# Three of four gate projections by seven products, norm's weights spread by TensorE, and three token blocks side by side

## The chip, the cores and the metric

The kernel runs on one core of one Trainium2 chip. The metric is the time of one execution on the device in microseconds, as the median of several. A core has the engines TensorE (matmuls, with the weight load as a step of its own), VectorE, ScalarE, GpSimd and SyncE, which here issues all DMAs. TensorE writes to PSUM, eight banks of 128 x 512 fp32 in this kernel; everything else lies in SBUF or in DRAM.

## The reference, cut to what matters

One decoder layer on 1024 tokens of width 1024. A norm, one wide input projection, two token mixers (attention, and a chunked state space scan, here SSD), a gated merge:

```
h = x * rsqrt(mean(x*x) + EPS) * norm_w                      # 1024 x 1024
q, k, v, z_a, xBC, z_s, dt, gates = split(h @ w_in)          # z_s: 2048 columns, four groups of 512
y_a = diff_attention(q, k, v) * silu(z_a)
y_s = group_rms_norm(ssd(silu(conv(xBC)), softplus(dt)) * silu(z_s))
merged = sigmoid(g_a) * (y_a @ w_proj_attn) + sigmoid(g_s) * (y_s @ w_proj_ssd)
out = x + merged @ w_out
```

The change concerns z_s, the 1024 x 2048 projection whose silu gates the scan's output, and norm_w.

## The kernel before

**Number format.** Every fp32 operand of a large matmul is split into a high and a low part, and a product is three matmuls, high-high, high-low and low-high (`steps3`, L557). For a weight block this means a ScalarE copy to the high part and a subtraction for the low part on VectorE or GpSimd, called a split below (`w_splits`, L424).

**Order.** No engine's order is left to a scheduler. A planner in the kernel's own Python (`Plan`, L79) holds an estimated time for each engine, runs generators as tasks, and so writes the instructions of all engines in one fixed order; each engine then works off its own list and waits where its data are not there. `bulk` (L1757) gives the order of TensorE's large pieces, `ORDER1` (L351): z0, dt, z1, then pairs of conv blocks (c), pairs of gate blocks (g), z2 and z3 between them, then eight attention heads (h), the remaining gates, the three merge products and the last projection. The SSD scan runs beside it as 32 chunks (four groups of eight), one every SLOW = 40 planned us in the front part and every PACE = 20 later.

**A plain z.** `ssd_proj_z(g)` (L1200) holds the eight weight blocks of 128 rows x 512 columns in eight of nine weight slots, and takes the eight token blocks one after the other: 8 row blocks x 3 matmuls into one PSUM bank, then silu on ScalarE and a store (`z_evac`, L1210). A weight slot is given back only after its use by the last token block.

**Seven products.** The pairs c and g already use Strassen-Winograd's form with seven half-size products instead of eight (`front_pair`, L1069; `ORDER`, L1456): the token halves of h are combined into four summed forms once (`form_evac`, L586), the weight quarters into sums on GpSimd (`pair_splits`, L452), and the products are added up in SBUF and PSUM. A pair's matmul has weights as the stationary and 512 tokens as the moving operand.

**Buffers.** Four raw buffers for loaded weights, nine weight slots, 17 big and 16 middle ones in SBUF, eight PSUM banks. SSD may hold up to ten of the middle ones. The loader (`w_loads`, L380) takes buffers and issues loads in the list's order, so that a load that can't get its buffer holds up all later ones; ScalarE and VectorE work off the splits in the same order.

**The start.** `start` (L1778) loads the first x block in two halves, norm_w as two broadcasts of 512 columns to 128 partitions (`nwb`), and four weight blocks. `prep_h` (L632) takes each x block through the norm (VectorE multiplies by the row's scale and nwb, L659), eight transposes on TensorE, and `h_evac` writes the high and the low part.

Of the kernel before, what the change touches and what calls it, by code (L numbers as in the profile page):

```python
# [27 lines left out]
C_B = C_XBC + 2048  # L28
C_C = C_B + 512
C_ZS = 7168  # L30
# [109 lines left out]
def tile_hybrid_layer(ctx: ExitStack, tc: tile.TileContext, x, norm_w, w_in, q_norm_w, k_norm_w,  # L140
# [22 lines left out]
    cv_d = dram.tile([3072, S], F32, name="cv_d")  # L163
    z_d = dram.tile([GROUPS, S, 512], F32, name="z_d")
    t_d = dram.tile([12, 2, P, S], F32, name="t_d")

# [182 lines left out]

    CONV = (16, 20, 0, 2, 4, 6, 18, 22, 8, 10, 12, 14)  # L350
    ORDER1 = [("z", 0), ("dt", 0), ("z", 1)]  # L351
    for i in range(12):
        ORDER1 += [("c", CONV[i])] + ([("g", i - 1)] if i % 2 else [])
        if i in ZF:
            ORDER1.append(("z", ZF[i]))
    FPAIRS = [i for i in ORDER1 if i[0] in "cg"]
    ORDER1.append(("setup", 0))
    for h in range(HEADS):
        ORDER1.append(("h", h))
        if h in ZH:  # L360
            ORDER1.append(("z", ZH[h]))

    wlist = []
    for kind, i in ORDER1:
        if kind in "cg":
            wlist.append(pair_w(w_in, 0, (C_XBC if kind == "c" else C_GATE) + i * P))
        elif kind != "setup":
            wlist += att_w(i) if kind == "h" else wide_w(w_in, C_ZS + i * 512) if kind == "z" else block_w(w_in, KB, C_DT, SH)
# [11 lines left out]
    def w_loads(lo, hi):  # L380
        for i in range(lo, hi):
            if isinstance(wlist[i], list) and isinstance(wlist[i][0], list):
                ks, raw, at = [], [], []
                for u in range(2):
                    for q in range(4):
                        ks.append((yield from pl.get(mids if u else raws)))
                    raw += [midt([P, 4, P], name=f"rawp{i}{q}") if u else
                            rpool.tile([P, 4, P], F32, tag="raw", name=f"rawp{i}{q}") for q in range(4)]
                    at += [load(raw[u * 4 + q], wlist[i][u][q // 2][:, :, q % 2 * P:(q % 2 + 1) * P]) for q in range(4)]
                raw_of[i] = (raw, ks, at)  # L390
                continue
            if isinstance(wlist[i], list):
                ks = yield from pl.get(raws, 4)
                raw = [rpool.tile([P, 4, P], F32, tag="raw", name=f"rawf{i}{q}") for q in range(4)]
                raw_of[i] = (raw, ks, [load(raw[q], wlist[i][q // 2][:, :, q % 2 * P:(q % 2 + 1) * P]) for q in (0, 1, 2, 3)])
                continue
# [27 lines left out]
    def w_splits():  # L424
        for i in range(len(wlist)):
# [5 lines left out]
            if isinstance(wlist[i], list):  # L431
                yield from pair_splits(*raw_of.pop(i), "G" if i < NFRONT else "V")
                continue
            k = yield from pl.get(ws)
# [17 lines left out]
    def pair_splits(raw, ks, at, eng):  # L452
# [33 lines left out]
        raws.give(ks[2], t)  # L486
        raws.give(ks[3], max(t, t22))

    def pairs_splits(raw, ks, at):
# [142 lines left out]
    def prep_h(t):  # L632
# [22 lines left out]
        pts = []  # L655
        nt = []
        for i in range(2):
# [400 lines left out]

    cv_at, z_at, ssd_n = {}, {}, {}

    def front_form(f, i):
# [5 lines left out]
    def front_pair(kind, b, last):  # L1067
# [6 lines left out]
        cell = {"kc": (yield from pl.get(mids)), "x": x, "ks": ks}  # L1074
        step = conv_step if kind == "c" else gate_step
        for n, (f, p) in enumerate(ORDER):
# [17 lines left out]
            w_done(ids[n])  # L1094
            pl.spawn(step(b, p, into[p], cell), pe_done())

# [10 lines left out]

    def gate_out(row, h, src, o, k, at):
        yield at
        at = act(o, src, AF.Tanh, at, scale=0.5)  # L1110
        t = at
        yield at
        at = load(gt_d[row * P:(row + 1) * P, h * 512:h * 512 + 512], o, at)
        mids.give(k, at)
        return t

    def gate_step(b, p, ps, cell):
        at = pe_done()
# [3 lines left out]
        elif p == 2:  # L1122
            k = yield from pl.get(mids)
            t = yield from gate_out(b, 0, ps, midt(name="go"), k, at)
            trs.give(kx, t)
        elif p == 4:
            c = cell["c"]
            at = tt(c, c, ps, ALU.add, max(at, cell["u", 7][2]))
            trs.give(ky, at)
            yield from gate_out(b + 1, 0, c, c, cell["kc"], at)  # L1130
        else:
# [5 lines left out]
            if p == 3:  # L1137
                trs.give(kz, at)
            yield from gate_out(b + (p == 5), 1, u, u, k, at)

# [59 lines left out]
    def ssd_proj_z(g):  # L1200
        ids = w_next(KB)
        for t in range(NT):
            k = yield from pl.get(trs, first=True)
            pm = mmt(f"pmz{g}{t}")
            yield from proj_tok(pm, t, ids, t == NT - 1)
            pl.spawn(z_evac(g, t, pm, k), pe_done())
            if g == 0 and t == 0:
                pl.spawn(consts())
# [15 lines left out]
    def ssd_core(g):  # L1224
# [532 lines left out]
    def bulk():  # L1757
        pl.spawn(ssd_all())
        pl.spawn(prepare())
        step = {"z": ssd_proj_z, "h": att_proj}  # L1760
        for kind, i in ORDER1:
            if kind in "cg":
                yield from front_pair(kind, i, (kind, i) == FPAIRS[-1])
            elif kind in step:
                yield from step[kind](i)
            else:
                yield from dt_proj() if kind == "dt" else att_setup()
        pl.spawn(fill())
        yield from gates()
        lag[:] = [0.0135, 2.5]  # L1770
        for c in range(3):
            yield from products(c)
        yield from final()

    kn = [mids.take() for _ in range(2)]
    nwb = [midt(name=f"nwb{i}") for i in range(2)]

    def start():  # L1778
        load_x(0)
# [11 lines left out]
        while len(h_at) < 2 * NT:  # L1791
            yield pl.t + 1.0
        for k in kn:
            mids.give(k, pl.t)

    def rest():
# [35 lines left out]
```

## Time and profile before

| | |
|---|---|
| median of 3 runs (lowest, highest) | 1624.73 us (1622.62, 1625.15) |
| the profiled execution's own time | 1625.04 us |
| its span in the trace | 1623.3 us |
| TensorE busy | 1589.2 us, 98% of the span |
| weight loads busy | 1330.2 us, 82% |
| VectorE, ScalarE, GpSimd busy | 1088.5, 915.1, 706.9 us |

The span runs from the first to the last instruction of one profiled execution; the own time holds 1.7 us around it. Busy time of TensorE is that of overlapping matmuls, so the pace of a stream is read from the starts of its matmuls and not from their durations. PE is TensorE, PEld its weight load, DVE VectorE, ACT ScalarE, POOL GpSimd, SP SyncE; a releaser is what an instruction waited for.

### The profile page before, as it was taken

The page shows a single profiled execution, that of the slowest core. Times are in us where ns is not written, and L with a number is a line of the kernel's source. Part 1 is how long each engine was busy: PE and PEld are TensorE (multiplying, and loading weights), DVE is VectorE, ACT ScalarE, POOL GpSimd, SP SyncE. Part 2 cuts the span into 40 slices and gives each one's busy share as a digit, 9 for nine tenths or more (in the row PEclk, how much of TensorE's full clock was granted, in tenths as well). Part 3 has the DMA queues.
Part 4 walks back from the last instruction along what each step waited for, and adds up shares of the span by engine and source line. Part 5 has one row for each costly group of instructions (what it writes and reads, how often), then busy time and mean ns, then how long its engine had stood idle before and what let it go on. Part 6 is the DMA issues. An engine that isn't in the chain of part 4 may idle for free.

```text
span 1623.3 us, 24344 instructions
## 1 busy us (share of the span) xinstructions
PE 1589.2 (98%) x8010; PEld 1330.2 (82%) x8010; DVE 1088.5 (67%) x2011; ACT 915.1 (56%) x2215; POOL 706.9 (44%) x847
## 2 busy tenths in 40 slices
PE   7999999999999999999989999999999999999999
PEld 5788888888788888887878888887887888888887
DVE  7836567537782576876767777876556577798831
ACT  7534447445563475786766777776666565352220
POOL 4315445334542543546475746464756433323000
PEclk9999999999999999999999999999999999999999
DMA  6213343533453461425163432433426397698941
GB/s 210 92 55 105 112 145 111 168 101 114 125 168 107 121 183 61 131 79 182 40 207 128 145 90 85 120 101 103 155 80 206 99 310 253 207 340 254 317 153 65
DMA packets 223804, 236.47 MB, mean 146 GB/s; under 512 B 15285, under 2 KB 155326, under 8 KB 223678
## 3 DMA queue, kind: packets, MB, share of 16 engines
q1 hardware_dynamic: 223678, 234.93, 45.6%
q8 instruction: 63, 1.03, 0.3%
q14 instruction: 63, 0.52, 0.1%
HBM read 164.48 MB, written 70.39 MB: 145 GB/s over the span
## 4 chain that ended last, share of the span: by engine, by line
PE 73%; DVE 3%; ACT 2%; POOL 2%; DMA 2%; issue 1%; SPq 0%; POOLq 0%; DVEq 0%; ACTq 0%
PE pma L199 18%; PE py L199 6%; PE pmz L199 5%; PE po L199 5%; PE pO L199 4%; PE pz L199 4%; PE px L199 4%; PE sc L199 4%; PE av L199 4%; PE fYc L199 3%; PE fXc L199 2%; PE pg L199 2%; PE pa L208 2%; PE fZc L199 2%; PE fYg L199 1%; PE pS L199 1%
## 5 line engine op out<-in xcount | busy, mean ns | idle before, releaser
L199 PE MATMUL pma<-w,hH 128*128 128x512 f32 x1024 | 345.2, 405 | 6.0 <-POOL w L233 5.4
L199 PEld LDWEIGHTS pma<-w,hH 128*128 128x128 f32 x1024 | 188.6, 189 | 40.9 <-POOL w L233 6.6
L199 PE MATMUL pma<-w,hL 128*128 128x512 f32 x512 | 206.8, 404 | 0.0
L199 PE MATMUL pmz<-w,hH 128*128 128x512 f32 x512 | 164.1, 398 | 0.7 <-ACT hH L225 0.7
L233 POOL TENSOR_TENSOR rawf<-rawf,rawf 128x512 f32<-128x512 f32 x54 | 71.6, 1326 | 166.4 <-DVE wp L233 87.8
L225 ACT ACTIVATE p<-p,nm 128x256 f32<-128x256 f32 (+7 forms) x128 | 98.6, 773 | 33.6 <-DVE nm L831 32.9
L225 ACT ACTIVATE w<-raw 128x512 fp32r<-128x512 f32 (+1 forms) x122 | 75.1, 626 | 75.0 <-DMA raw<-in_w_in_dram 28.7
L199 PEld LDWEIGHTS pmz<-w,hH 128*128 128x128 f32 x512 | 96.5, 190 | 20.6 <-ACT hH L225 1.1
L199 PEld LDWEIGHTS pma<-w,hL 128*128 128x128 f32 x512 | 96.8, 189 | 16.4
L233 POOL TENSOR_TENSOR w<-raw,w 128x512 fp32r<-128x512 f32 (+1 forms) x38 | 51.3, 1351 | 134.5 <-ACT w L225 120.7
L199 PE MATMUL fYc<-ft,wp 128*128 128x512 f32 x432 | 106.5, 392 | 0.7 <-DVE fu L233 0.7
L199 PE MATMUL pmz<-w,hL 128*128 128x512 f32 x256 | 101.4, 396 | 0.0
L199 PEld LDWEIGHTS fYc<-ft,wp 128*128 128x128 f32 x432 | 81.1, 189 | 17.9 <-DVE fu L233 1.1
L225 ACT ACTIVATE wp<-rawp 128x512 fp32r<-128x512 f32 x72 | 44.2, 626 | 84.1 <-POOL rawp L233 23.9
L233 DVE TENSOR_TENSOR wp<-rawf,wp 128x512 fp32r<-128x512 f32 x72 | 59.1, 837 | 34.7 <-ACT wp L225 34.7
L233 DVE TENSOR_TENSOR w<-raw,w 128x512 fp32r<-128x512 f32 (+1 forms) x84 | 65.1, 782 | 23.5 <-ACT w L225 23.3
L225 ACT ACTIVATE ab<-ab,nac 128x128 f32<-128x128 f32 x256 | 78.4, 392 | 1.7 <-POOL ab L1234 1.5
L199 PEld LDWEIGHTS av<-v,at 128*128 128x128 f32 x576 | 72.8, 191 | 6.5 <-ACT at L225 2.6
L265 POOL TENSOR_TENSOR rs<-rs,mhalf 128x4 f32<-128x4 f32 (+1 forms) x71 | 75.4, 1062 | 5.9
L225 ACT ACTIVATE wp<-rawf 128x512 fp32r<-128x512 f32 x108 | 65.9, 626 | 20.0 <-POOL rawf L233 16.4
L199 PE MATMUL av<-v,at 128*128 128x128 f32 x576 | 75.1, 275 | 1.7 <-ACT at L225 1.7
L831 DVE CUSTOM_DVE_ANT_0 p<-sc,maskb 128x512 f32<-128x512 f32 (+3 forms) x128 | 72.1, 584 | 6.2 <-PE sc L199 3.9
(299 smaller groups left out, 4217.8 us busy)
## 6 DMA issues: line engine op xcount, KB each, us to landing
raw<-in_w_in_dram SPq DMA_DIRECT2D x104, 256.0 KB, 3.6
rawf<-in_w_in_dram SPq DMA_DIRECT2D x72, 256.0 KB, 3.7
ab<-act_d SPq DMA_DIRECT2D x32, 512.0 KB, 4.9
cv_d<-cv SPq DMA_DIRECT2D x48, 256.0 KB, 2.1
t_d<-ts SPq DMA_DIRECT2D x24, 512.0 KB, 3.1
z_d<-zs SPq DMA_DIRECT2D x32, 256.0 KB, 2.0
xr<-cv_d SPq DMA_DIRECT2D x32, 256.0 KB, 3.0
zc<-z_d SPq DMA_DIRECT2D x32, 256.0 KB, 3.0
```

What stands on the lines that cost most here:

```text
L199: nc.tensor.matmul(o, lhsT=lhsT, rhs=rhs, start=start, stop=stop, **kw)
L208: nc.tensor.transpose(out=o, in_=i, identity=ident if idn is None else idn)
L225: nc.scalar.activation(o, i, f, **kw)
L233: (nc.vector if eng == "V" else nc.gpsimd).tensor_tensor(out=o, in0=a, in1=b, op=op)
L265: nc.gpsimd.tensor_tensor(out=dst, in0=dst, in1=mhalf[:, 0:cols], op=ALU.pow)
L831: nc.vector.tensor_tensor_reduce(out=p[:, j:e], in0=sc[i][:, 0:e - j], in1=maskb[:, S - n + j:S - n + e], scale=-1.0, scalar=nms[i - 1] if ...
```

## The change

z1, z2 and z3 are computed with seven products of 512 tokens x 512 rows x 256 columns each; z0 stays plain (`PLAIN`). Here the tokens are the stationary operand and 256 columns of the weights the moving one, since the result is wanted with tokens on partitions. A product's weight block comes as two halves of 256 rows (`tok_w`, `tok_splits`), 14 in all, from eight loads of which four go to raw and four to middle buffers. `tok_unit` runs the products, `tok_step` adds them up and stores. z2 and z3 come earlier in the order by two c pairs and one g pair each (`FRONT_ORDER`). PACE becomes 21. SSD starts a group when its z has been stored by the plan's time instead of when its stores are planned.

norm_w comes as two rows of 512 in one partition, and TensorE spreads them over the partitions by a matmul of full fp32 with a column of ones into two PSUM banks, which are held until all of h is made.

In z0 the last three token blocks run side by side: for each weight block three token blocks, in three banks.

Some parts that the diff also names are not used here (`za_d`, `v_d`, the kinds a and v).

```diff
-PACE = 20
+PACE = 21
-ZF, ZH = {5: 2, 9: 3}, {}
+FRONT_ORDER = "z0 d0 z1 c16 c20 g0 c0 c2 g2 z2 c4 c6 g4 c18 c22 g6 z3 c8 c10 g8 c12 c14 g10"
+PLAIN = (("z", 0),)
...
+    def tok_w(c0):
+        return tuple(w_in[kh * 512 + kp * 256:kh * 512 + kp * 256 + 256, c0 + r * 256:c0 + r * 256 + 256]
+                     .rearrange("(k p) c -> p k c", p=P) for kp in range(2) for kh in range(2) for r in range(2))
...
+            if isinstance(wlist[i], tuple) and len(wlist[i]) == 8:
+                ks = yield from pl.get(raws, 4)
+                raw = [rpool.tile([P, 2, 256], F32, tag="raw", name=f"rawt{i}{q}") for q in range(4)]
+                at = [load(raw[q], wlist[i][q]) for q in range(4)]
+                km = yield from pl.get(mids, 4)
+                raw += [midt([P, 2, 256], name=f"rawt{i}{q}") for q in range(4, 8)]
+                at += [load(raw[q], wlist[i][q]) for q in range(4, 8)]
...
+    def tok_splits(raw, ks, km, at):
+        a11, a21, a12, a22 = [[raw[q], raw[4 + q]] for q in range(4)]
+        kt = yield from pl.get(mids, 2)
...
+        for kp in range(2):
+            yield t0[kp]
+            t3.append(tt(s3[kp], a11[kp], a21[kp], ALU.subtract, t0[kp], "G"))
+            t1.append(tt(a21[kp], a21[kp], a22[kp], ALU.add, t0[kp], "G"))
+        u11 = yield from split(a11, t0, "V")
+        for kp in range(2):
+            t2.append(tt(a11[kp], a21[kp], a11[kp], ALU.subtract, max(t1[kp], u11[kp]), "G"))
+        yield from split(a11, t2, "V")
+        u12 = yield from split(a12, t0, "V")
+        for kp in range(2):
+            t4.append(tt(a12[kp], a12[kp], a11[kp], ALU.subtract, max(t2[kp], u12[kp]), "G"))
...
+        t = yield from split(s3, t3, "G")
...
+        t = yield from split(a21, t1, "V")
...
+        t = yield from split(a22, t0, "G")
...
+        t = yield from split(a12, t4, "G")
...
+        while "nwb" not in ready:
+            yield pl.t + 0.1
...
+    def tok_unit(kind, g, last):
+        ids = w_next(14)
...
+        for n, (f, p) in enumerate(ORDER):
+            for b in range(2 * ((into[p], 0) not in ps)):
+                k = yield from pl.get(trs, first=True)
+                ps[into[p], b] = (trt(f"t{into[p]}{kind}{g}{b}"), k)
+            for kp in range(2):
+                yield from w_need(ids[2 * n + kp])
+                if f[0] == "t":
+                    while any(("formed", t) not in ready for t in range(4, NT)):
+                        yield pl.t + 0.2
...
+                for j in range(4):
+                    b = j // 2
+                    while kp == 0 and p in BEFORE and (("c22", b) if p == 3 else (BEFORE[p], b)) not in cell:
+                        yield pl.t + 0.1
+                    o = ps[into[p], b][0][:, j % 2 * 256:j % 2 * 256 + 256]
+                    for kk in range(2):
+                        hf = front_form(f, 2 * kp + kk)
+                        yield from steps3(o, [a[:, j * P:(j + 1) * P] for a in hf], (wt[:, 0, kk], wt[:, 1, kk]),
+                                          kp + kk == 0 and p in (1, 6, 5) and j % 2 == 0, kp + kk == 2, skip_group_check=True)
+                    if kp and j % 2:
+                        pl.spawn(tok_step(kind, g, p, b, ps[into[p], b], cell), pe_done())
+                w_done(ids[2 * n + kp])
...
+    def tok_step(kind, g, p, b, bank, cell):
...
+        if p == 1:
+            k = yield from pl.get(mids)
+            c = midt(name=f"tc{b}")
+            cell["ct", b] = (c, k, act(c, ps, AF.Copy, at))
+        elif p in (6, 7):
...
+            cell[("u", p), b] = (u, k, tt(u, cell["ct", b][0], ps, ALU.add, at))
+        elif p == 2:
+            k = yield from pl.get(mids)
+            yield from out(ps, midt(name="to"), k, at, True)
+        elif p == 4:
+            c, k, t = cell["ct", b]
+            at = tt(c, c, ps, ALU.add, max(at, t, cell[("u", 7), b][2]))
+            trs.give(kb, at)
+            yield from out(c, c, k, at, False)
...
     def ssd_proj_z(g):
         ids = w_next(KB)
-        for t in range(NT):
+        for ts in ((0,), (1,), (2,), (3,), (4,), (5, 6, 7)):
...
-        while any(cv_at.get(i, INF) > pl.t for i in need) or any((g, t) not in z_at for t in range(NT)):
+        while any(cv_at.get(i, INF) > pl.t for i in need) or any(z_at.get((g, t), INF) > pl.t for t in range(NT)):
...
-    kn = [mids.take() for _ in range(2)]
-    nwb = [midt(name=f"nwb{i}") for i in range(2)]
+    kn, kb_ = [mids.take() for _ in range(2)], [trs.take() for _ in range(2)]
+    nwr = [midt([1, 512], name=f"nwr{i}") for i in range(2)]
+    nwb = [trt(f"nwb{i}") for i in range(2)]
+    one = const.tile([1, P], F32, name="one")
+    nc.gpsimd.memset(one, 1.0)
+
+    def norm_rows(t):
+        yield t
+        for i in range(2):
+            mm(nwb[i], one, nwr[i], True, True)
+        ready["nwb"] = pe_done()
...
-            load(nwb[i], norm_w[:, i * 512:i * 512 + 512].partition_broadcast(P).rearrange("p a d -> p (a d)"))
+            t = load(nwr[i], norm_w[:, i * 512:i * 512 + 512])
+        pl.spawn(norm_rows(t), t)
```

## Rows read from the trace of the kernel before

**Rows 1.** The page: each engine's busy us, share of the span, instructions.

```profile
PE 1589.2 (98%) x8010; PEld 1330.2 (82%) x8010; DVE 1088.5 (67%) x2011; ACT 915.1 (56%) x2215; POOL 706.9 (44%) x847
```

**Rows 2.** Waits of TensorE: total us, times, longest us.

```profile
PE pma L199 <- POOL w L233: 5.4, 3, 2.3
PE pO L199 <- DVE cv L241: 2.5, 1, 2.5
```

**Rows 3.** Timeline of z0 (start us, us): 28 rounds of three lie between.

```profile
40.38 0.61 PE L199 MATMUL pmz<-w,hH 128*128 128x512 f32 x2
...
59.42 0.61 PE L199 MATMUL pmz<-w,hH 128*128 128x512 f32 x2
```

**Rows 4.** Timeline of 256-column matmuls; tile view of their loads (ns min/median/max).

```profile
1615.39 0.88 PE L199 MATMUL po<-w,hH 128*128 128x256 f32 x6
...
1616.11 0.88 PE L199 MATMUL po<-w,hL 128*128 128x256 f32 x6
...
L199 PEld LDWEIGHTS po<-w,hH x204: 187/188/192, 1532.5 to 1619.8; 128*128 128x128 f32 x102
```

**Rows 5.** Groups of the pairs' weights; DMA issues with us to landing.

```profile
L225 ACT ACTIVATE wp<-rawf 128x512 fp32r<-128x512 f32 x108 | 65.9, 626 | 20.0 <-POOL rawf L233 16.4 <-PE pmz L199 2.6 <-DMA rawf<-in_w_in_dram 0.2
L233 DVE TENSOR_TENSOR wp<-rawf,wp 128x512 fp32r<-128x512 f32 x72 | 59.1, 837 | 34.7 <-ACT wp L225 34.7
L233 POOL TENSOR_TENSOR rawf<-rawf,rawf 128x512 f32<-128x512 f32 x54 | 71.6, 1326 | 166.4 <-DVE wp L233 87.8 <-issue 43.9 <-PE fYc L199 13.1
...
rawf<-in_w_in_dram SPq DMA_DIRECT2D x72, 256.0 KB, 3.7
```

**Rows 6.** Busy us in z2: PE, PEld, DVE, ACT, POOL; clock, DMA, GB/s.

```profile
301.50:350.20 48.70, 48.70 (x231) 40.66 (x230) 13.95 (x23) 24.07 (x47) 12.41 (x13) 1.00 0.38 121
```

**Rows 7.** Timeline of the start; busy us there (columns as in rows 6).

```profile
2.63 2.01 SPq L254 DMA_DIRECT2D raw<-in_w_in_dram  x4
3.56 0.63 ACT L225 ACTIVATE hL<-x 128x512 fp32r<-128x512 f32 x1 [1.50 <-DMA x<-in_x_dram]
6.76 0.75 DVE L241 SCALAR_TENSOR_TENSOR x<-x,rs,nwb 128x512 f32<-128x512 f32 x1 [1.54 <-DMA nwb<-in_norm_w_dram]
...
5.00:10.00 5.00, 2.23 (x8) 1.43 (x8) 2.35 (x4) 1.18 (x3) 0.55 (x1) 1.00 0.95 322
10.00:15.00 5.00, 4.36 (x10) 3.34 (x11) 3.79 (x7) 4.51 (x10) 0.81 (x2) 1.00 0.80 228
```

**Rows 8.** The norm's multiplications: all 16, and beside GpSimd; a PSUM input.

```profile
L241 DVE SCALAR_TENSOR_TENSOR x<-x,rs,nwb 128x512 f32<-128x512 f32 x16 | 13.7, 894 | 4.8 <-POOL rs L265 2.8 <-DMA nwb<-in_norm_w_dram 2.0
...
29.36 2.44 DVE L241 SCALAR_TENSOR_TENSOR x<-x,rs,nwb 128x512 f32<-128x512 f32 x2
29.78 3.17 POOL L233 TENSOR_TENSOR r<-hH,hL 128x512 f32<-128x512 f32 x2
...
1603.63 0.69 DVE L241 SCALAR_TENSOR_TENSOR xr<-po,xr 128x512 f32<-128x512 f32 x1 [4.75 <-PE po L199]
```

**Rows 9.** Tile views (ns min/median/max, first and last start us); ScalarE's timeline.

```profile
L233 DVE TENSOR_TENSOR ft<-r,ft x16: 408/420/1518, 53.6 to 72.6; 128x256 fp32r<-128x256 f32 x16
L199 PE MATMUL pdt<-hH,w x16: 387/390/396, 66.9 to 74.1; 128*64 128x512 f32 x16
62.34 0.31 ACT L225 ACTIVATE w<-raw 128x128 fp32r<-128x128 f32 x1 [4.91 <-PE pmz L199]
```

**Rows 10.** Timeline of two matmuls in full fp32.

```profile
95.80 0.59 PE L199 MATMUL pacum<-tv,tri 128*128 128x256 f32 x2
96.23 0.59 PE L199 MATMUL pacum<-tv,ones 128*128 128x256 f32 x2
```

**Rows 11.** Tile views: SSD's first and last transposes, attention's projections.

```profile
L208 PE MATMUL px<-ident,xr x128: 270/272/328, 241.6 to 1079.3; 128*128 128x128 f32 x128
L208 PE MATMUL py<-ident,xn x128: 270/272/328, 266.1 to 1111.6; 128*128 128x128 f32 x128
L199 PE MATMUL pma<-w,hL x512: 387/393/775, 598.3 to 1238.9; 128*128 128x512 f32 x171
```

More of the change, by code (lines that the diff above doesn't have):

```diff
@@ L348, in pair_w @@
                 for q in range(2)]
[L350 to L356, printed above, removed]
+    ORDER1 = []
+    for e in FRONT_ORDER.split():
+        ORDER1.append((e[0], int(e[1:])))
+    FPAIRS = [i for i in ORDER1 if i[0] in "cgazv" and i not in PLAIN]
     ORDER1.append(("setup", 0))
@@ L432, in w_splits @@
                 yield from pair_splits(*raw_of.pop(i), "G" if i < NFRONT else "V")
+                continue
+            if isinstance(wlist[i], tuple) and len(wlist[i]) == 8:
+                yield from tok_splits(*raw_of.pop(i))
                 continue
@@ L487, in pair_splits, with split @@
         raws.give(ks[3], max(t, t22))
+    def tok_splits(raw, ks, km, at):
+        a11, a21, a12, a22 = [[raw[q], raw[4 + q]] for q in range(4)]
+        kt = yield from pl.get(mids, 2)
+        s3 = [midt([P, 2, 256], name="s3") for _ in range(2)]
+        def split(src, ts, eng):
+            done = []
+            for kp in range(2):
+                k = yield from pl.get(ws)
+                n = made[0]
+                made[0] += 1
+                wt = wpool.tile([P, 2, 2, 256], F32R, tag="w", name=f"wt{n}")
+                yield ts[kp]
+                t = act(wt[:, 0], src[kp], AF.Copy, ts[kp])
+                yield t
+                t = tt(wt[:, 1], src[kp], wt[:, 0], ALU.subtract, t, eng)
+                wts[n], w_at[n], w_slot[n] = wt, t, k
+                done.append(t)
+            return done
+        t0 = [max(at[0:4]), max(at[4:8])]
+        t3, t1, t2, t4 = [], [], [], []
+        for kp in range(2):
[9 more added lines that the diff above has]
+            t4.append(tt(a12[kp], a12[kp], a11[kp], ALU.subtract, max(t2[kp], u12[kp]), "G"))
+        raws.give(ks[0], t4[0])
+        mids.give(km[0], t4[1])
+        t = yield from split(s3, t3, "G")
+        for kp in range(2):
+            mids.give(kt[kp], t[kp])
+        t = yield from split(a21, t1, "V")
+        raws.give(ks[1], t[0])
+        mids.give(km[1], t[1])
+        t = yield from split(a22, t0, "G")
+        raws.give(ks[3], t[0])
+        mids.give(km[3], t[1])
+        t = yield from split(a12, t4, "G")
+        raws.give(ks[2], t[0])
+        mids.give(km[2], t[1])
     def pairs_splits(raw, ks, at):
@@ L1074, in front_pair @@
         cell = {"kc": (yield from pl.get(mids)), "x": x, "ks": ks}
[L1075 removed]
+        if kind == "c":
+            step, how = conv_step, ()
+        else:
+            step, how = gate_step, ((AF.Tanh, 0.5, gt_d) if kind == "g" else (AF.Silu, 1.0, za_d),)
         for n, (f, p) in enumerate(ORDER):
@@ L1129, in gate_step @@
             trs.give(ky, at)
-            yield from gate_out(b + 1, 0, c, c, cell["kc"], at)
+            yield from gate_out(b + 1, 0, c, c, cell["kc"], at, how)
         else:
@@ L1138, in gate_step @@
                 trs.give(kz, at)
-            yield from gate_out(b + (p == 5), 1, u, u, k, at)
+            yield from gate_out(b + (p == 5), 1, u, u, k, at, how)
+    def tok_unit(kind, g, last):
+        ids = w_next(14)
+        ps = {}
+        into = {1: "x", 6: "y", 2: "x", 7: "y", 5: "z", 4: "y", 3: "z"}
+        cell = {}
+        for n, (f, p) in enumerate(ORDER):
+            for b in range(2 * ((into[p], 0) not in ps)):
+                k = yield from pl.get(trs, first=True)
+                ps[into[p], b] = (trt(f"t{into[p]}{kind}{g}{b}"), k)
+            for kp in range(2):
+                yield from w_need(ids[2 * n + kp])
+                if f[0] == "t":
+                    while any(("formed", t) not in ready for t in range(4, NT)):
+                        yield pl.t + 0.2
+                    at = max(ready["formed", t] for t in range(4, NT))
+                    if at > pl.t:
+                        yield at
+                wt = wts[ids[2 * n + kp]]
+                for j in range(4):
[10 more added lines that the diff above has]
+                w_done(ids[2 * n + kp])
+            if last and f[0] == "t":
+                for part in range(2):
+                    for kp in range(2):
+                        bigs.give(forms_t[f, part, kp][1], pl.t + 0.1)
@@ L1201, in ssd_proj_z @@
         ids = w_next(KB)
-        for t in range(NT):
[L1203 to L1207, printed above, removed]
+        for ts in ((0,), (1,), (2,), (3,), (4,), (5, 6, 7)):
+            pms = []
+            for t in ts:
+                k = yield from pl.get(trs, first=True)
+                pms.append((mmt(f"pmz{g}{t}"), k))
+            for kb in range(KB):
+                yield from w_need(ids[kb])
+                for t, (pm, k) in zip(ts, pms):
+                    while (t, kb // 4) not in h_at:
+                        yield pl.t + 0.1
+                    while h_at[t, kb // 4] > pl.t:
+                        yield h_at[t, kb // 4]
+                    hb = hH[:, kb, t * P:(t + 1) * P], hL[:, kb, t * P:(t + 1) * P]
+                    yield from steps3(pm, hb, wide(ids[kb]), kb == 0, kb == KB - 1)
+                    if kb == KB - 1:
+                        pl.spawn(z_evac(g, t, pm, k), pe_done())
+                if ts[-1] == NT - 1:
+                    w_done(ids[kb])
+            if g == 0 and ts[0] == 0:
                 pl.spawn(consts())
@@ L1761, in bulk @@
         for kind, i in ORDER1:
-            if kind in "cg":
+            if kind in PAIR_C:
                 yield from front_pair(kind, i, (kind, i) == FPAIRS[-1])
+            elif kind in TOK_C and (kind, i) not in PLAIN:
+                yield from tok_unit(kind, i, (kind, i) == FPAIRS[-1])
             elif kind in step:
@@ L1766, in bulk @@
             else:
-                yield from dt_proj() if kind == "dt" else att_setup()
+                yield from dt_proj() if kind == "d" else att_setup()
         pl.spawn(fill())
@@ L1792, in start @@
             yield pl.t + 1.0
-        for k in kn:
+        for k, b in zip(kn, kb_):
             mids.give(k, pl.t)
+            trs.give(b, pl.t)
     def rest():
```

66 lines of the change are left out of this document (56 added, 10 removed).

## The prediction

> **What bounds the kernel now.** I read the page first: TensorE is busy 98% of the span, VectorE 67%, ScalarE 56% [rows 1]. Then the waits of TensorE: the two largest after the start are three stops for a GpSimd split, 5.4 us in all, and one of 2.5 for VectorE [rows 2]. The rest is a stream of matmuls whose pace decides. So I read the pace: in the first z, 28 rounds of three 512-column matmuls go from 40.38 to 59.42, 0.680 a round, 0.2267 us each [rows 3]. A change helps by taking columns from TensorE, by shortening the start, or by removing stops; it hurts by new stops.
>
> **Seven products: the columns.** A plain z is 8 token blocks x 8 row blocks x 3 high-low terms = 192 matmuls of 512 columns, 192 x 0.2267 = 43.5 us. In the new unit each of seven products is 2 halves x 4 token blocks x 2 row blocks x 3 terms = 48 matmuls of 256 columns, 336 in all. Columns fall to 7/8, but a matmul costs more than its columns: at 512 it takes 0.2267 where 512/2.4 GHz is 0.2133. The price at 256 stands at the end of the trace, where the last token block runs in two parts of 256 with the same high-low order and a weight load before each: six in 0.72 us (1615.39 to 1616.11), 0.120 each [rows 4]. So 336 x 0.120 = 40.3 us, 3.2 saved a group, **9.6 us for three groups**. An eighth of the time would be 5.4 a group and 16.3 for three; four tenths of it go into the price that each matmul has beside its columns. Bounds: a weight load shows 0.188 us, longer than the 0.120 in which a matmul with its load is done [rows 4], so the loads overlap, with little slack; 1% more a matmul would be 1.2 us for three groups, so I keep 8.4 to 9.6.
>
> **Seven products: the other engines.** A z of old needs 8 splits (ScalarE copy, VectorE or GpSimd subtraction) and 8 evictions on ScalarE. A new one needs 14 splits, 8 sums on GpSimd, and for evictions 10 operations on ScalarE and 10 on VectorE. Priced by the pairs' rows (copy 0.63, also for an eviction; subtraction on VectorE 0.84; GpSimd 1.33, also for its 6 subtractions) [rows 5] and by 0.69 for a VectorE eviction [rows 8]: ScalarE gains 8 x 0.63 = 5.0 us; VectorE has 8 x 0.84 + 10 x 0.69 = 13.6 where it had two thirds of 8 subtractions, 4.5, so +9.1; GpSimd has 14 x 1.33 = 18.6 where it had the other third, 3.6, so +15. In the old z2, with SSD beside it, they are busy 24.07, 13.95 and 12.41 of 48.7 us [rows 6]: all fits under the matmuls, cost 0 in the sum. Without that cover GpSimd's 18.6 would be the longest of the three. In a pair one product of 12 matmuls, 12 x 0.2267 = 2.7 us, lies between a product and the one that waits for its sum; here one of 48 x 0.120 = 5.8 us, so I expect fewer stops of this kind. The z loads stay 8 of 256 KB with shorter rows; the pairs' loads, whose rows are shorter still, land in 3.7 us [rows 5], so 0. The stores stay 8 per group.
>
> SBUF — State Buffer of the Trainium skill (section "SBUF: two separate sides") speaks against this part: a VectorE operation with two SBUF inputs and a GpSimd operation that reads SBUF take one shared port pair in turn, whole instructions at a time. The trace agrees: two VectorE operations, 0.75 us each alone, took 2.44 beside GpSimd sums [rows 7, 8]. At the rule's worst VectorE would also stand still for GpSimd's whole 18.6 us, would then have 14 + 9.1 + 18.6 = 42 us in a unit of about 45, and the sum could be 1 us a group worse. By the row of the same subtraction, 0.837 in the mean, the loss is small and in the price that I used.
>
> **z1 at third place.** Its second product needs the summed token forms. Their last operation starts at 72.6, and dt's last matmul starts at 74.1 [rows 9]. z1 would start about 2 us earlier than now, near 72.4, and its second product 5.8 later, at 78: 5 us to spare. Its raw halves need all four raw buffers, which now wait for dt's second split; that one waits for a weight slot until 62.34, with ScalarE standing still behind it for 4.91 us [rows 9]. With the last three blocks side by side the first slot comes free after 9 matmuls of a 72-matmul stretch, 14.3 us before z0's end at 66.9, that is at 52.6: 9.7 us earlier. This part buys no TensorE time itself; it pays for z1's supply. From 53: 8 loads at 0.5 an issue and 3.7 to land [rows 5, 7], 7.7 us; four sums 5.3, two more 2.6, copies and subtractions 2 x (0.63 + 0.84) = 2.9; the second product's halves are there at 71.5. Cost 0, bounds 0 to 6 (all of z1's lead lost).
>
> **Norm's weights.** Two broadcasts of 256 KB leave. VectorE waits for the first until 6.76 [rows 7]. The new rows of 2 KB are issued at the same place, right behind the two halves of the first x block, the first of which is in use at 3.56 [rows 7]; two or three issues of 0.5 later, I take 4.3. Then two matmuls in full fp32: 256 columns took 0.43 (95.80 to 96.23), 512 cost 0.86 at this clock [rows 10]. TensorE here is at the lower of its levels: from 10 to 15 us it shows ten matmuls of 512 in 4.36 us, and 512/1.2 GHz is 0.427 [rows 7]; so 1.7 us each, done at 6.0 and 7.7. VectorE can begin 0.7 us sooner, while the first transposes, now queued behind both matmuls, can't: they begin at 7.7, where now they follow VectorE's 6.76 + 0.75. Gain comes from behind: 0.52 MB at the 322 GB/s of 5 to 10 us [rows 7] is 1.6 us less in front of the weights and all x blocks. And the 16 multiplications read PSUM as one input: an operation of this kind with a PSUM input takes 0.69, these took 0.894 on average, 2.44 for two beside GpSimd [rows 8]: 16 x 0.2 = 3.3 us on VectorE, for whose blocks the first z waits. The matmuls could also bring the clock up sooner: ten matmuls of 10 to 15 us would then cost 0.227 each and 2 us less, as far as the weights' splits allow. Bounds: 1 us lost (rows landing at 5.5) to 4 won; I take **2 won**.
>
> **Order and pace.** z2 and z3 each move two conv pairs and one gate pair earlier; no work is added, and z2 now meets SSD's first chunk. PACE 21 lengthens SSD's end by at most 23 chunks x 1 us: its last transpose is at 1111.6, the last attention projection at 1238.7 [rows 11], 127 us later. Cost 0. But all later order shifts, and the old stops (5.4 and 2.5 us, [rows 2]) may vanish or others come: -7 to +6, taken as 0.
>
> **Rooms that shrink.** The unit takes two PSUM banks at a time, and the first pair is free again before the third is asked for: four at once. Of the 16 middle buffers it takes 4 raw, 2 sums, 2 + 4 partial results, up to 2 outputs. I put 1 us of stops on this.
>
> **Sum.** 1625.04 (the profiled execution) - 9.6 - 2 + 1 = 1614.4, so **1614**. The median shown is 1624.73, 0.3 lower; the difference is below what I can resolve.
>
> **Rivals.**
> *Forecast, 0.60*: 1608 to 1620.
> *Late halves, partly covered, 0.14*: stops of 5 to 10 us in all, 1618 to 1626, centre 1622. For it: 14 splits through the same 9 slots; against it: pairs already draw a split every 2.7 us and TensorE rarely stops.
> *Slower, by the middle buffers before z3, 0.12.* The loader asks for four at once, with SSD holding its share. Supply takes 7.7 + 5.3 + 2.6 + 2.9 = 18.5 us; the unit before (84 x 0.2267 = 19.0) and the first product (5.8) give 24.8, so up to 6.3 us of waiting is free. An SSD chunk holds buffers for 24.5 us (the first from 241.6 to 266.1 [rows 11]) of each 40. If the four wait for its end, 18.2 us are lost at z3 alone: 1614.4 + 18.2 = 1632.6. It makes the kernel slower from a wait of 6.3 + 10.6 + 3.2, about 20 us. Against it: one chunk uses 8 of 16.
> *More, 0.11*: a start 4 us shorter and the old stops gone: 1625.04 - 9.6 - 4 - 7 = 1604.4, centre 1605.
> *The weight load sets the pace, 0.03*: if each of 336 loads cost its 0.188, a group is 63.2 us, +19.7, and the run 1625.04 + 59 - 1 = 1683. [Rows 4] deny it, but only on 48 matmuls with idle neighbours. TensorE: Matmul & The Clock Gate of the Trainium skill ("LDWEIGHTS (loading the stationary operand)") gives columns/1.2 ns, an estimate of 107 ns for 128 columns: unhidden behind 256 columns it would be worse still, hidden it is just covered. The trace agrees with the second.
>
> Within 0.2% (3.2 us) a measurement of this kernel can't tell a change: the limits are 1621.5 and 1628. Faster: 0.60 + 0.11 + 0.05 of the late halves = 0.76; same 0.08; slower 0.01 + 0.12 + 0.03 = 0.16. The range goes from the "more" case to the edge of the late halves, which is also the sum with its costs at their upper bounds (1625.04 - 8.4 + 1 + 1 + 6 = 1624.6): 1605 to 1625; the forecast's own is 1608 to 1620.
>
> **What would show it.** z1 to z3 as 336 matmuls at 0.120, each unit near 40.3 us plus what SSD interleaves; the first z's transposes at 7.6 and dt ending near 72; the multiplications at 0.69; no wait of the units on ScalarE copies or VectorE sums over 1 us. Wrong would be: more than 0.126 a matmul, stops on split halves at z1's second product or z3's first, or a later first transpose. Behind norm's two matmuls TensorE holds the first transposes and, behind those, the first z; VectorE holds all splits behind the first multiplication: a late row would show in both.

## The result

The changed kernel takes 1603.87 us (median of 4 runs, 1601.88 to 1607.26), the kernel before 1623.67 measured beside it (4 runs, 1620.62 to 1625.15). The ratio is 0.9883, with a 95% interval of 0.9860 to 0.9906: 19.8 us faster, almost twice what was forecast, and 1.1 us below the range. The profiled execution took 1603.58, its span is 1601.6, 21.7 less than before.

**Where the 21.7 us are.** The page, which answers to [rows 1], shows TensorE as the bound as before:

```profile
PE 1578.4 (99%) x8446; PEld 1341.7 (84%) x8446; DVE 1119.3 (70%) x2049; ACT 925.9 (58%) x2239; POOL 749.5 (47%) x882
```

The start. The timeline shows the two matmuls that spread norm's weights, the first multiplications and transposes; the last fence has dt's matmuls, which answer to [rows 9]:

```profile
4.07 3.75 PE L203 MATMUL nwb<-nwr,one 1*128 1x512 f32 x4 [4.07 <-DMA nwr<-in_norm_w_dram]
6.24 0.75 DVE L245 SCALAR_TENSOR_TENSOR x<-x,rs,nwb 128x512 f32<-128x512 f32 x1 [1.27 <-PE nwb L203]
7.75 2.03 PE L212 MATMUL ph<-ident,x 128*128 128x128 f32 x8
7.86 0.75 DVE L245 SCALAR_TENSOR_TENSOR x<-x,rs,nwb 128x512 f32<-128x512 f32 x1 [0.88 <-PE nwb L203]
```

```profile
L203 PE MATMUL pdt<-hH,w x16: 387/390/396, 64.5 to 71.7; 128*64 128x512 f32 x16
```

dt begins at 64.5 where it began at 66.9: 2.4 us won. From there on the view of windows gives, for before and for the changed kernel, the length and TensorE's busy time (columns as in [rows 6]):

```profile
66.90:1623.30 1556.40, 1532.84 (x7753) 1285.39 (x7751) 1034.09 (x1924) 870.40 (x2123) 677.88 (x809) 1.00 0.46 146
```

```profile
64.50:1601.60 1537.10, 1519.71 (x8185) 1296.43 (x8183) 1067.26 (x1963) 882.68 (x2151) 721.52 (x843) 1.00 0.47 147
```

TensorE stands idle 1556.4 - 1532.8 = 23.6 us in the one and 17.4 in the other. Counted one by one, the stops before matmuls (0.05 us and more, from dt's start on) are 20.5 and 14.2; the rest are shorter ones. The granted clock is at the lower level, 1.2 GHz, for 6.8, 3.4 and 3.4 us of this stretch before, and for 3.4 and 3.4 after. The windows around these places show it, before and then changed:

```profile
418.00:427.00 9.00, 7.77 (x28) 6.92 (x29) 5.61 (x11) 2.59 (x6) 1.27 (x2) 0.62 0.86 238
845.00:850.00 5.00, 3.72 (x14) 3.04 (x15) 4.08 (x6) 4.92 (x11) 3.31 (x3) 0.66 1.02 335
1257.00:1263.00 6.00, 4.98 (x16) 3.93 (x17) 5.21 (x12) 1.18 (x3) 5.62 (x4) 0.72 1.14 341
```

```profile
694.00:701.00 7.00, 5.36 (x22) 4.62 (x23) 3.14 (x7) 6.57 (x20) 2.24 (x5) 0.76 0.60 196
825.00:831.00 6.00, 5.67 (x25) 4.72 (x26) 1.50 (x3) 4.93 (x17) 5.76 (x8) 0.72 0.88 272
```

At half clock about half the time is lost, counted here as 13.6 / 2 = 6.8 us before and 3.4 after. What is left is TensorE's own work: 1556.4 - 20.5 - 6.8 = 1529.1 and 1537.1 - 14.2 - 3.4 = 1519.4 (from unrounded figures). So 21.7 is **2.4 at the start, 9.7 of work, and 9.6 of stops and halved clock**. TensorE: Matmul & The Clock Gate of the Trainium skill (section "HAM oscillation — how this bites in real kernels") also counts half of the throttled time as lost; the trace agrees nearly: a matmul of 512 columns takes 0.427 us in these stretches and 0.2267 otherwise, 47% lost.

**The units.** Product after product of 48 matmuls takes 5.76 us, 0.120 a matmul, and the three units lie in windows almost without idle time (timeline, then windows; 231 matmuls of the old z2 are in [rows 6]):

```profile
90.01 5.92 PE L203 MATMUL tyz<-wt,ft 128*128 128x256 f32 x48
95.77 5.92 PE L203 MATMUL tzz<-wt,ft 128*128 128x256 f32 x48
```

```profile
71.90:114.80 42.90, 42.90 (x358) 42.48 (x357) 33.26 (x48) 22.47 (x36) 23.87 (x19) 1.00 0.24 69
229.00:273.00 44.00, 44.00 (x368) 43.84 (x367) 20.00 (x29) 28.19 (x54) 25.41 (x21) 1.00 0.43 124
403.20:449.70 46.50, 46.50 (x382) 45.97 (x381) 26.85 (x40) 26.29 (x52) 26.58 (x23) 1.00 0.38 114
```

**The stops** are others than those of [rows 2]. The waits of TensorE in the changed kernel:

```profile
PE av L203 <- ACT at L229: 2.9, 1, 2.9
PE pS L203 <- ACT at L229: 2.1, 1, 2.1
PE px L212 <- DVE qk L237: 1.9, 1, 1.9
PE pma L203 <- POOL w L237: 0.5, 2, 0.4
```

The 5.4 us for GpSimd's splits and the 2.5 for a conv block are gone, and stops in attention stand in their place. No line of the diff changes the work at either place. So the open question was whether the order and PACE make the kernel better, or whether any change deals the stops anew.

### The profile page after: what moved, and what is told of

Read it like the earlier page. It is cut to its first block, busy times and chain, and to the rows that moved or that the text cites. A ratio compares the mean times of both kernels' runs of the same rounds, so it can differ in the third digit from the quotient of the medians.

```text
span 1601.6 us, 25383 instructions
## 1 busy us (share of the span) xinstructions
PE 1578.4 (99%) x8446; PEld 1341.7 (84%) x8446; DVE 1119.3 (70%) x2049; ACT 925.9 (58%) x2239; POOL 749.5 (47%) x882
## 4 chain that ended last, share of the span: by engine, by line
PE 85%; ACT 6%; POOL 3%; DVE 2%; DMA 2%; issue 1%; SPq 0%; POOLq 0%; DVEq 0%; ACTq 0%
PE pma L203 16%; PE py L203 6%; PE fYc L203 6%; PE po L203 5%; PE px L203 4%; PE pz L203 4%; PE fXc L203 4%; PE fZc L203 4%; PE pO L203 4%; PE av L203 3%; PE sc L203 3%; PE tyz L203 3%; PE fYg L203 3%; PE pg L203 3%; PE txz L203 2%; PE fZg L203 2%
## 5 line engine op out<-in xcount | busy, mean ns | idle before, releaser
L229 ACT ACTIVATE p<-p,nm 128x512 f32<-128x512 f32 (+7 forms) x128 | 98.6, 772 | 14.9 <-DVE nm L903 10.2
L229 ACT ACTIVATE w<-raw 128x512 fp32r<-128x512 f32 (+1 forms) x98 | 60.7, 626 | 60.3 <-PE po L203 22.9
L237 POOL TENSOR_TENSOR w<-raw,w 128x512 fp32r<-128x512 f32 (+1 forms) x30 | 39.2, 1308 | 94.6 <-ACT w L229 79.6
L266 POOL TENSOR_SCALAR rs<-ss 128x4 f32<-128x4 f32 (+1 forms) x71 | 21.2, 298 | 122.0 <-DVE ss L828 101.9
L237 POOL TENSOR_TENSOR rawp<-rawp,rawp 128x512 f32<-128x512 f32 x36 | 52.7, 1475 | 52.3 <-DVE wp L237 37.6
L203 PE MATMUL sc<-kk,qh 128*128 128x512 f32 (+2 forms) x192 | 66.7, 354 | 0.4 <-DVE kk L237 0.4
L237 DVE TENSOR_TENSOR w<-raw,w 128x512 fp32r<-128x512 f32 (+1 forms) x68 | 57.3, 852 | 9.5 <-ACT w L229 9.0
```

Of the source, the lines that this page charges most:

```text
L203: nc.tensor.matmul(o, lhsT=lhsT, rhs=rhs, start=start, stop=stop, **kw)
L229: nc.scalar.activation(o, i, f, **kw)
L237: (nc.vector if eng == "V" else nc.gpsimd).tensor_tensor(out=o, in0=a, in1=b, op=op)
L266: nc.gpsimd.tensor_scalar(out=dst, in0=src, scalar1=add, scalar2=None, op0=ALU.add)
```

## The experiments

Three theories. **Pace** (theory 1): PACE 21 spreads the scan better. **Order** (theory 3, or B for g1 to g4): the new places of z2 and z3 keep the scan and the pairs apart. **Deal** (theory 2, or A): each shift of the written order moves all later meetings of the engines' lists, so stops come and go with no relation to what was changed, and the change's own worth is only work and start. "Left" in the table is the span from dt's start less stops and half of the halved clock, worked out as above; the front ends with the first projection of attention. Ratios are against the kernel before, measured beside each (1623.31 to 1624.06). Stops and clock are those of one profiled execution: runs of one kernel spread by 1 to 10 us, and the longer ones mostly have the lower mean clock.

| kernel | median us | ratio (95%) | dt starts | stops, front / later | half of halved clock | left |
|---|---|---|---|---|---|---|
| before | 1623.67 | 1 | 66.9 | 4.6 / 15.9 | 6.8 | 1529.1 |
| e1 before, PACE 21 | 1617.59 | 0.9959 (0.9947, 0.9972) | 68.2 | 4.5 / 9.0 | 5.1 | 1528.9 |
| e3 changed, every z plain | 1628.55 | 1.0025 (1.0013, 1.0037) | 63.9 | 9.5 / 12.7 | 10.2 | 1529.1 |
| e4 before, norm's rows | 1618.22 | 0.9966 (0.9954, 0.9978) | 63.9 | 4.6 / 14.5 | 1.7 | 1530.0 |
| g3 before, SLOW 41 | 1624.04 | 1.0008 (0.9998, 1.0017) | 68.7 | 4.3 / 13.7 | 5.1 | 1529.9 |
| changed | 1603.87 | 0.9883 (0.9860, 0.9906) | 64.5 | 2.2 / 12.1 | 3.4 | 1519.4 |
| e2 changed, PACE 20 | 1594.57 | 0.9818 (0.9804, 0.9831) | 64.9 | 2.0 / 6.2 | 0 | 1519.7 |
| f1 e2, old places | 1630.90 | 1.0046 (1.0032, 1.0060) | 65.1 | 14.3 / 19.0 | 10.2 | 1520.0 |
| f2 e2, one by one | 1625.41 | 1.0005 (0.9993, 1.0018) | 64.5 | 8.5 / 17.3 | 13.7 | 1518.5 |
| f3 e2, broadcasts | 1598.36 | 0.9846 (0.9828, 0.9865) | 67.3 | 2.5 / 6.2 | 0 | 1519.9 |
| f4 changed, PACE 19 | 1605.72 | 0.9893 (0.9874, 0.9912) | 64.5 | 2.3 / 14.7 | 1.7 | 1519.8 |
| g1 e2, SLOW 41 | 1615.77 | 0.9957 (0.9942, 0.9971) | 64.3 | 10.2 / 13.1 | 5.1 | 1520.6 |
| g2 f1, SLOW 41 | 1609.67 | 0.9918 (0.9899, 0.9937) | 64.2 | 9.0 / 10.8 | 1.7 | 1521.0 |
| g4 e2, SLOW 38 | 1627.95 | 1.0025 (1.0012, 1.0037) | 65.1 | 18.5 / 12.6 | 10.2 | 1519.9 |

The five kernels with plain z have 1528.9 to 1530.0 left, mean 1529.4; the nine with units 1518.5 to 1521.0, mean 1519.9. Stops and halved clock together are 19 to 32 us with plain z and 8 (e2) to 44 (f1) with units, with means of 24.5 and 25.3: within this spread no stops show that the units as such bring or take. "Left" is good to about 1 us: where a stretch of halved clock begins inside a stop, as in f2, up to 1.2 us stand in both columns. Counted once, the means are 1529.7 and 1520.3, and their difference 9.4 instead of 9.5.

The start has a spread of its own: e1 and g3 start as the kernel before does, and their dt begins at 68.2 and 68.7 where its begins at 66.9. The four kernels with broadcasts have 67.8 in the mean, the ten with norm's rows 64.5.

**e1: the kernel before with the new PACE.**

```diff
-PACE = 20
+PACE = 21
```

> The kernel before with PACE 21 and nothing else. If the pace takes TensorE's stops in the attention part away (theory 1), the three stops of projections for a GpSimd split (5.4 us) shrink below 1.5 and the run is 4 to 7 us faster than before, 1617 to 1620. If the stops come and go with any shift of the written order (theory 2), the time is within 4 us of before in either direction and the stops stand at other places, with a sum of 10 to 20 us as before. If the pace does nothing (theory 3, the front's order brings the rest), 1623 to 1625.

6.5 us faster: 6.9 of stops in attention and gates went, the front stayed. Taken alone it speaks for "pace"; it is 2.5 us more than theory 2 allowed.

**e2: the changed kernel with the old PACE.**

```diff
-PACE = 21
+PACE = 20
```

> The changed kernel with PACE back at 20. Theory 1: 4 to 7 us slower than the changed kernel, 1608 to 1611, with stops of projections for GpSimd splits again. Theory 2: within 4 us of 1604 either way, and this difference is not the mirror image of that of PACE 21 in the kernel before. Theory 3: 1603 to 1605.

9.3 us faster than the changed kernel, so the same step has the other sign here. That is against theory 1, and also more than twice the 4 us that theory 2 allowed. It beats both kernels, with the least stops of all and no halved clock after the start; its largest waits and its mean clock:

```profile
PE nwb L203 <- DMA nwr<-in_norm_w_dram: 4.1, 1, 4.1
PE fXg L203 <- ACT fc L229: 1.5, 2, 1.0
...
PE py L212 <- ACT yt L229: 1.0, 1, 1.0
```

```profile
core 0: 1592.8 us, clock 1.000
```

**e3: the changed kernel with every z plain**, at the new places, norm's rows and side by side kept.

```diff
-PLAIN = (("z", 0),)
+PLAIN = (("z", 0), ("z", 1), ("z", 2), ("z", 3))
```

> The changed kernel with all four z plain; order, pace, norm rows and side by side stay. TensorE's own time for a plain z is 43.5 us and for a unit 40.3, so by columns alone this is 9.6 us slower than the changed kernel, 1613 to 1614. If the units also take stops away (or the plain ones bring some), it is 13 us or more slower, 1617 and up; if units cost stops of their own, 1611 or less.

24.7 us slower than the changed kernel. Only 9.7 of them are in "left"; 14.7 are stops and halved clock (32.4 against 17.7), and none of the larger stops is a z's: they are waits of attention and of the scan. So the time is that of the expected case in which the units take stops away, but no wait of a z shows it.

**e4: the kernel before with norm's rows alone.** `nwb` is two PSUM banks written by `norm_rows`, as in the diff of the change; nothing else.

```diff
-    nwb = [midt(name=f"nwb{i}") for i in range(2)]
+    nwr = [midt([1, 512], name=f"nwr{i}") for i in range(2)]
+    nwb = [trt(f"nwb{i}") for i in range(2)]
```

> The kernel before with norm's weights as two rows spread by TensorE, nothing else. By the start alone dt begins 2.0 to 2.5 us sooner than 66.9 (the changed kernel: 64.5) and the run is 2 to 3 us faster, 1621 to 1622. By theory 2 the later stops are dealt anew by the shift and the run lies anywhere within 4 us of that, though dt begins at 64.5; if side by side is what moved dt, dt begins at 66.9 here.

dt begins 3.0 us earlier, at 63.9. The run is faster by 5.8, the profiled execution by 8.7: 3.0 of start, 1.5 of stops, and 5.1 of halved clock, less 0.9 that "left" is longer. The stop of 2.5 us near 419 is still there, but 3.4 us at half clock follow it instead of 6.8. The stretches near 846 and 1259 don't come, though the stop at the first place is still 1.5 us (2.4 before) and that at the second 1.9 (2.0 before). So some 3.4 of the 5.1 us come with nearly the same stops, in this one execution.

**f1: e2 with z2 and z3 at their old places.**

```diff
-FRONT_ORDER = "z0 d0 z1 c16 c20 g0 c0 c2 g2 z2 c4 c6 g4 c18 c22 g6 z3 c8 c10 g8 c12 c14 g10"
+FRONT_ORDER = "z0 d0 z1 c16 c20 g0 c0 c2 g2 c4 c6 g4 z2 c18 c22 g6 c8 c10 g8 z3 c12 c14 g10"
```

> Base for this and the next two is the changed kernel with PACE 20, 1594.6 us, whose profile shows 2.0 us of TensorE's stops from dt to the end of the front part, 6.2 after it, and no stretch at the halved clock. Here z2 and z3 go back to their old places. If the order brought the missing gain (theory 3), the front part gets its 2.5 us stop and a halved clock back and the run is 5 to 8 us slower than the base, near 1601. If stops are dealt anew by any shift (theory 2), the columns' part of the front keeps its value (front part without stops and halved clock 512 to 513 us from dt's start), and only stops and clock differ: 1592 to 1606.

36.3 us slower than e2, far more than any theory gave: 25.0 of stops, 10.2 of halved clock, and the work the same. With 14.3 us of stops in the front it looked like "order":

```profile
PE fYg L203 <- DVE fu L237: 4.7, 2, 3.1
PE pa L212 <- DVE p L245: 4.0, 5, 2.0
PE pO L203 <- DVE ab L237: 3.2, 2, 3.0
...
PE pO L203 <- DVE cv L245: 3.2, 1, 3.2
```

None of these is a wait of a unit on its own supply.

**f2: e2 with z0's last token blocks one after the other.**

```diff
-        for ts in ((0,), (1,), (2,), (3,), (4,), (5, 6, 7)):
+        for ts in ((0,), (1,), (2,), (3,), (4,), (5,), (6,), (7,)):
```

> The base with the last token blocks of the first z one after the other. If side by side pays for z1's supply, as predicted, dt's second split again waits for a slot that comes 9.7 us later, z1's halves come late, and TensorE stops before z1's first or second product: 3 to 10 us between dt's start and the end of z1 over the base. If the supply has slack enough, that stretch is within 0.5 us of the base and the run within 4 us of it, by whatever stops the shift deals.

z1's first product stops for its own weights, and the clock falls during the stop (timeline, two lines of it with three matmuls from one to the next, then window):

```profile
73.18 0.39 PE L203 MATMUL txz<-wt,hH 128*128 128x256 f32 x1
76.52 0.58 PE L203 MATMUL txz<-wt,hH 128*128 128x256 f32 x1 [2.96 <-DVE wt L237]
```

```profile
77.54 0.41 PE L203 MATMUL txz<-wt,hL 128*128 128x256 f32 x1
78.18 0.41 PE L203 MATMUL txz<-wt,hL 128*128 128x256 f32 x1
```

```profile
71.90:86.00 14.10, 10.76 (x71) 10.31 (x71) 12.30 (x17) 5.35 (x9) 6.25 (x5) 0.76 0.13 42
```

The stop is 3.0 us. Of the 6.8 at half clock some 2 lie in the stop, and in the other 4.8 a matmul takes 0.213 us instead of 0.120, which costs 2.1. From dt's start to the end of z1 it is 56.3 us where e2 has 50.4: 5.9 us, inside the 3 to 10 expected. That is what side by side is worth here. The other 25 of 30.8 us are stops and halved clock elsewhere, many times the 4 that the expectation gave to a shift.

**f3: e2 with norm's weights as two broadcasts again** (the reverse of e4's edit).

> The base with norm's weights by two broadcasts as before. Additive: dt starts 2.4 to 3.0 us later, near 67.5, and the run is 2.5 to 3 us slower than the base, near 1597. If the start's gain is side by side's work, dt starts within 0.5 us of the base's 64.9. Theory 2 allows 4 us more or less behind that.

3.8 us slower, dt 2.5 later. Here the later order kept its stops (6.2 both times), and the part shows its own worth.

**f4: the changed kernel with PACE 19.**

```diff
-PACE = 21
+PACE = 19
```

> The changed kernel with PACE 19: no work changes, only where SSD's chunks fall in the attention part. Theory 1 in its reverse form (a denser SSD is better for the new kernel): 1588 to 1594. Theory 2 (a new deal of the same stops): anywhere from 1592 to 1606, with the front part as in the base to 0.5 us and the whole difference in stops and halved clock behind it.

PACE 19, 20 and 21 give 1605.72, 1594.57 and 1603.87, with the front equal (2.0 to 2.3 us of stops) and 14.7, 6.2 and 12.1 later. "Pace" falls: both neighbours of 20 are slower here, and on the kernel before 21 was the faster one.

**g1 to g4: one planned us more or two less between the scan's chunks in the front**, no work and no place changed: g1 and g4 on e2, g2 on f1, g3 on the kernel before.

```diff
-FRONT, SLOW = 12, 40.0
+FRONT, SLOW = 12, 41.0
```

> Theory A (the stops are dealt anew by every shift of the written order, whatever makes it): no work is changed, TensorE's time without stops and halved clock stays within 1 us of the changed kernel's with PACE 20, but its 2 us of stops between dt and attention become anything from 2 to 14 and clock dips of 3.4 may come; 1595 to 1625. Theory B (the new places of z2 and z3 themselves keep the front free of stops): stops in the front stay at or below 5 us, 1591 to 1603.

> The units at the old places, with the scan's chunks in the front one planned us further apart. Theory A: the 14.3 us of stops in the front that the old places showed are one deal of many and change by more than 5 us, down to some 5 to 9 with fewer dips; 1605 to 1625. Theory B (at the old places the units run into the scan and the pairs): stops in the front stay above 11 us, 1622 to 1638.

> The kernel before, with the scan's chunks in the front one planned us further apart. Theory A: the same columns, stops in the front between 2 and 14 us where they were 4.6, other dips; 1615 to 1640, and the time without stops and dips as before within 1 us. Theory B (stops belong to the design): the front's stops stay within 2 us of 4.6, the run within 5 us of the kernel before.

> As the run with 41, other direction: 38 planned us between chunks. Theory A: stops in the front anywhere from 2 to 14 us, 1595 to 1625, not in step with the 41. Theory B: at or below 5 us, 1591 to 1603.

On e2, 41 costs 21.2 us and 38 costs 33.4, with 10.2 and 18.5 us of stops in the front where there were 2.0; 38 goes beyond theory A's own bounds of 14 us and 1625 too. Each of these kernels keeps its own time from run to run (g1 1614.36 to 1618.56, g2 1608.39 to 1610.18, g4 1627.34 to 1629.48), so the difference belongs to the written order and not to the single execution. On f1, 41 wins 21.2: the old places then give 1609.67, faster than the new places in g1 and g4. "Order" as told falls: the places by themselves keep the front neither free nor full. g3 tells nothing apart: on the kernel before the time stayed, as theory B had it, and lies in A's wide bounds too. The stops did change there: the one of 2.5 us near 419 is gone and one of 3.2 came at 461.8, with nearly the same sum in the front (4.3 for 4.6). So it isn't excluded that the units make the order more sensitive to a shift than plain z do. The largest waits of g2, against f1's above:

```profile
PE fXg L203 <- ACT fc L229: 4.5, 2, 2.9
...
PE fYg L203 <- DVE fu L237: 3.5, 2, 3.1
```

How such a stop comes about, in g4's timeline of all engines (other lines left out):

```profile
391.94 0.27 PE L212 MATMUL pb<-ident,bT 128*128 128x128 f32 x1
...
395.15 0.74 DVE L245 SCALAR_TENSOR_TENSOR cv<-fXc,cols,cv 128x509 f32<-128x509 f32 x1
...
395.99 0.63 ACT L229 ACTIVATE cv<-cv 128x512 f32<-128x512 f32 x1 [2.08 <-DVE cv L245]
396.52 0.26 ACT L229 ACTIVATE bT<-pb 128x128 fp32r<-128x128 f32 x1
...
396.68 0.30 ACT L229 ACTIVATE ch<-cT 128x128 fp32r<-128x128 f32 x1
...
397.03 0.80 PE L203 MATMUL pO<-sh,ch 128*128 128x512 f32 x1 [4.83 <-ACT ch L229]
```

The scan's matmul at 397.03 needs `ch`, which is 0.3 us of ScalarE's work. But in ScalarE's written list it stands behind the silu of a conv block, and that waits 2.08 us for VectorE, which is working off that block's taps one after the other. TensorE works off its own list in order and stands for 4.83. This is the scan's fourth chunk. In e2 the same chunk was written later, beside z3: no conv block stands just ahead of its `ch`, TensorE has a unit's matmuls to run meanwhile, and the chunk's matmul starts without a stop (g1 has it the same way, at 409.32):

```profile
407.84 0.30 ACT L229 ACTIVATE ch<-cT 128x128 fp32r<-128x128 f32 x1
410.77 0.40 PE L203 MATMUL pO<-sh,ch 128*128 128x512 f32 x1
```

This is shown for one stop; that the others come about in the same way was not followed one by one.

## Why the prediction was wrong, step by step

- **The start**, 2 us won: 2.4 measured, 3.0 with norm's rows alone (e4), 2.5 at dt in f3, 3.3 between the means of all kernels with and without rows. The rows were in use at 4.07 (4.3 taken), the first multiplication followed the first matmul at 6.24 (6.0 taken), the first transposes the second at 7.75 (7.7). The multiplications got faster, but less than the 0.69 taken: 743 ns in the mean where they had 894 [rows 8], 2.4 us in all instead of 3.3. Right; which of the step's sources of gain (fewer bytes, faster multiplications, a sooner clock) brought how much was not separated.

```profile
L245 DVE SCALAR_TENSOR_TENSOR x<-x,rs,nwb 128x512 f32<-128x512 f32 x16 | 11.2, 743 | 4.6 <-POOL rs L269 2.4 <-PE nwb L203 2.1
```

- **Seven products, the columns**, 9.6: 9.7 between the two profiled executions, 9.5 between the means of five and nine kernels. Right, and so is its price of 0.120 a matmul, taken from six matmuls at the end of the old trace [rows 4]. With it falls the rival of the weight load.
- **The other engines**, 0: no stop over 0.3 us in the three units. ScalarE's copies took the 626 ns expected; VectorE's subtractions 901 where 837 was taken, GpSimd's work 61.1 / 3 = 20.4 us a unit where 18.6 was taken. In z1 VectorE is busy 33.26 of 42.9 us: it still fits. The rivals of late halves and of middle buffers before z3 have nothing to show.

```profile
L237 POOL TENSOR_TENSOR rawt<-rawt,rawt 128x512 f32<-128x512 f32 x18 | 25.7, 1439 | 19.8 <-DVE wt L237 17.1 <-DMA rawt<-in_w_in_dram 2.3
L229 ACT ACTIVATE wt<-rawt 128x512 fp32r<-128x512 f32 x36 | 21.6, 626 | 16.4 <-POOL rawt L237 5.0 <-PE tyz L203 4.9 <-PE txz L203 4.5
L237 DVE TENSOR_TENSOR wt<-rawt,wt 128x512 fp32r<-128x512 f32 x24 | 21.2, 901 | 4.6 <-ACT wt L229 4.4
```

(GpSimd's 61.1 are these 25.7 and three smaller groups of 15.7, 10.0 and 9.7.)

- **z1 at third place**, 0 with side by side paying for its supply, 6 us at most without: f2 lost 5.9 us there. Right, though the wait was at the first product and not at the second.
- **Rooms that shrink**, +1: 0 measured.
- **Order and pace** is the step that failed: "the old stops ... may vanish or others come: -7 to +6, taken as 0". Measured: -9.6, of which 6.2 are stops and 3.4 halved clock. The mechanism was named, as others coming for those that vanish; its size was wrong twice. The step looked at the two largest groups of waits, four stops of 7.9 us in all, where the trace of before held 20.5 us of stops after dt and 13.6 us at half clock, for which the sum has no term: together 27.3 us that a new order could give back. Behind those two groups the list of waits of before goes on:

```profile
PE pc L199 <- ACT yt L225: 2.3, 1, 2.3
PE sc L199 <- DVE kk L233: 2.2, 2, 2.0
```

And the step drew its bounds from those four stops alone: the 14 kernels span 8 to 44 us, -19 to +16 against before. The rival "more" met the time (1604.4 against 1603.87) with a chance of 0.11, by luck: a start 1.6 us too large, stops nearly right, and no clock, so that the errors cancel. That the time lies 1.1 us out of the range says little, since its own runs span 5.4 us; that the order brought 9.6 where 0 was taken is the error.

So the change itself is worth 9.5 us of columns and 2.4 to 3.3 at the start, 12 to 13 us; the other 7 or 8 of the measured 19.8 belong to this written order. The experiments that show that an order alone can do this are g1, g2 and g4: they change no work and move the time by 21 to 33 us.

What stays open: how the 7 or 8 us divide between the new places, PACE and the new rule for a group's start (PACE 21 wins 6.5 us on one kernel and loses 9.3 on the other, and the rule has no run of its own), and which spacing a given kernel likes. No run here tells it ahead, and no version was tried that lets TensorE pass a chunk that isn't ready.

## What to carry to other kernels

In a kernel whose order is written out by hand, first take the trace apart into start, stops, halved clock and work; a change's own worth shows in the work (here 1529.4 against 1519.9, to about 1 us), while the median also holds a deal of stops that the change didn't make. Before a part is judged by one run, shift the order by something that does no work, as a planned interval, and see how far the time moves; and when a change is kept, try its neighbours, since here one gave 9.3 us more than the change as made. In a prediction the bounds of "the order shifts" come from the sum of all stops and of the halved clock, not from the largest few.

## What the runs showed of the hardware

The clock's fall is not tied to a stop of a certain length. Over the 14 profiled executions, of TensorE's stops after the first 35 us, a stretch at 1.2 GHz began in or within 4 us behind 5 of 29 stops of 1 to 1.5 us, 4 of 19 of 1.5 to 2, 9 of 14 of 2 to 2.5, 7 of 8 of 2.5 to 3, and all 12 above (where two stops lie so ahead of one stretch, both are counted). It lasted 3.4 us in most cases, 6.8 in others and 10.2 once; one stretch had no stop above 1 us so near ahead of it. Nearly the same stop had different sequels: the one of 2.5 us near 419 was followed by 6.8 us in the kernel before and by 3.4 in e4. The runs of the changed kernel, 1601.88 to 1607.26, had mean granted clocks of 0.999 and 0.996 at these two ends.

Half the clock costs a little less than half the time. In the stretches at 1.2 GHz matmuls of 512 and 256 columns follow each other at 0.427 and 0.213 us, which is their columns at that clock and nothing more; at 2.4 GHz they take 0.2267 and 0.120 where the columns alone would be 0.2133 and 0.1067. So the 13 ns that a matmul costs beside its columns show at the higher clock only, and the lower one costs 47% and 44% of the time spent in it.
